# Norm products, token-major transposes and softmax transposes written one projection later, and pinned in their place, in a two-layer hybrid backbone

## The chip, the cores and the metric

The kernel runs on one core of one Trainium2 chip. The metric is the device time of one execution in microseconds (us).

## What is computed

A stream of 512 latent tokens and 256 context tokens, 1024 channels wide, goes through two layers. In each, a modulated RMSNorm is followed by one wide input projection that feeds three mixers side by side, and by a squared-ReLU MLP. All values are float32; the large products are made as three products of rounded and remainder parts.

```
h    = rmsnorm(x) * (1 + sc) + sh
na_* , dn_*, z, fn_u, gate = split(h @ w_in)
o_na = softmax(q k_window^T + bias | q k_ctx^T) v        # 8 heads of 64, 8x16 window and all context
q,k  = rope(l2norm(silu(conv5(dn_q,k)))), v = silu(conv5(dn_v))
o_dn = headnorm(delta_rule_fwd + delta_rule_bwd) * silu(z)   # 4 heads of 128
o_fn = real(fft2(fn_u))
x    = x + gt1 * (sum_i sigmoid(gate_i) * (o_i @ w_i)) @ w_out
x    = x + gt2 * relu(norm(x) @ w1)^2 @ w2
```

The first layer computes latents and context (an "all" projection is 512 + 256 columns); in the second, queries, z and gates are needed for the latents alone.

## The kernel before

Weights come in blocks of 128 output channels. `wload` (L224) loads two halves of 256 KB on SyncE's queue, rounds them on ScalarE (`whi`, L232) and makes the remainder on GpSimd or VectorE (`wlo`, L235). `proj` (L239) runs 24 matmuls over the latents and 24 over the context (L244). `inproj` (L378) does one block of the input projection in one go; its two results take both buffers of PSUM tag `pl`.

Each layer has three parts: a Fourier part (head 0 of the delta rule runs beside it), the mixing part, and the rest (branch projections, output projection, MLP). The mixing part is four Python generators that `by_clock` (L329) interleaves while the program is written out: each `yield` tells how many units of a planned clock the step takes, and the stream with the earliest due time writes its next step.

- `stream_in`: the remaining projections, 40 per layer. A projection yields `IN_T`, 12 units in the first layer and 7 in the second. It picks attention inputs first, then delta heads (when the head two before is over), then z; a gate projection is put in at a fixed ratio.
- `stream_na`: attention, four blocks of two heads; `na_in` of the next block starts when the block before is done. `na_pair` (L786) is one tile of 128 queries: scores (yield 1), softmax (yield 3), transposes of the probabilities on TensorE (L814, yield 2), product with v (L820, yield 2). A block is six pairs in the first layer, four in the second.
- `stream_prep`: for one head after the other, the triangular inverses (`dn_prep`): products of k and q (L553, L555), 31 substitution steps on VectorE (L580, L582), two round trips through DRAM, four rounds of small matmuls, and the copy that ends it (L642). A head begins when its `qT` is written.
- `stream_dn`: the scan of each head (`dn_step`), then its output (`dn_out`, L725).

`dn_in` (L511) prepares one head: project k, convolution and SiLU (`conv_silu`, L455: evacuation L460, five VectorE steps, a sigmoid, the product L470), L2 norm and rotation (`l2_rope`, L473: square L476, product with ones on TensorE L481, four DMAs that swap rows, a product on GpSimd L493, the sum L495); then k's token-major transposes (`tok_major`, L504), project v, convolution; v's transposes, project q, convolution, L2 norm. The convolution's padded input `cin`, its result `y`, the square `r_l2` and a gate's `gl` all take buffers of SBUF tag `cy`, of which the mixing part has three (`mix_a`, L954).

The writing order is a priority, not the final order. When the program is built, a scheduler fills each engine's queue: of what it estimates to be ready, the earliest written goes first; `PRI` moves the delta scan 200 places forward in the first layer. On the chip each queue runs in the order so fixed, and an instruction waits at its head until its inputs are there. So a matmul that was put too early holds everything behind it on TensorE.

Of the kernel before, what the change touches and what calls it, by code (L numbers as in the profile page):

```python
# [17 lines left out]
P = 128  # L18
D = 1024
KD = 8  # L20
TL = 512
TC = 256
TT = TL + TC
# [9 lines left out]


IN_T, LAT_STEP, HEAD, PRI, GR, G0 = (12, 7), (2, 3), (5, 0), (200, 0), (0.5, 0.3), (0, 1)

ADA_G, ADA_BR, ADA_WO, ADA_M = 0.5, 0.3, 1.5, 0.95

# [4 lines left out]
V_N1, V_N2, V_BADA, V_CONV, V_DNN, V_LEN = 0, 8, 16, 64, 124, 125  # L43
# [3 lines left out]
def kernel(ctx: ExitStack, tc: tile.TileContext, A: dict, out: bass.AP):  # L47
# [316 lines left out]
    def layer(l):  # L364
# [13 lines left out]
        def inproj(t, sg):  # L378
# [13 lines left out]
                proj(pc, w, KD, hh, hl, sg[1:], TL, k0)  # L392
            return pl, pc

        def evac(dst, ps):
            act.copy(dst[:, 0:TL], ps[0])  # L396
            if ps[1] is not None:
                act.copy(dst[:, TL:TT], ps[1][:, 0:TC])
# [74 lines left out]
        def l2_rope(y, w, scale, name, par):  # L473
            n = 770 if w > TL else 512
            r = U("r_l2", tag="cy", w=774)
            act.activation(out=r[:, :n], in_=y[:, :n], func=AF.Square)  # L476
            for s0, s1, o0 in ((0, TL, 0), (TL, TT, 514)):
                if s0 < w:
                    o1 = o0 + s1 - s0
                    ps = ps_aux("ps_l2")  # L480
                    pe.matmul(ps[:, 0:s1 - s0], lhsT=ones, rhs=r[:, o0:o1], start=True, stop=True)  # L481
                    act.activation(out=r[:, o0:o1], in_=ps[:, 0:s1 - s0], func=AF.Ln, bias=EPS)
                    act.activation(out=r[:, o0:o1], in_=r[:, o0:o1], func=AF.Exp, scale=-0.5)
            o = U(name, tag=name + par)
# [12 lines left out]

        def tok_major(src, offs, name, tag):

            o = U(name, tag=tag).rearrange("p (j e) -> p j e", e=P)  # L500
            for j0, j1 in ((0, 4), (4, 6)):
                ps = ps_aux("ps_tm")
                for j in range(j0, j1):
                    pe.transpose(ps[:, (j - j0) * P:(j - j0 + 1) * P], src[:, offs[j]:offs[j] + P], ident)  # L504
                act.copy(o[:, j0:j1], ps[:, 0:(j1 - j0) * P].rearrange("p (j e) -> p j e", e=P))
            return o

# [1 line left out]
        OFFY = [j * P for j in range(4)] + [514, 642]  # L509

        def dn_in(h, st):  # L511
            y = conv_silu(inproj(T_DNK + h, ALL), V_CONV + 5 * (4 + h), TT)
            st["kT"] = l2_rope(y, TT, 1.0, "kT", str(h % 2))
            yield IN_T[l]
            st["ktok"] = tok_major(st["kT"], OFF, "ktok", f"ktok{h % 2}")
            y = conv_silu(inproj(T_DNV + h, ALL), V_CONV + 5 * (8 + h), TT)
            yield IN_T[l]
            st["vtok"] = tok_major(y, OFFY, "vtok", f"vtok{h % 2}")
            y = conv_silu(inproj(T_DNQ + h, segs), V_CONV + 5 * h, W)
            st["qT"] = l2_rope(y, W, float(P) ** -0.5, "qT", str(h % 2))  # L520
            yield IN_T[l]

        def dn_prep(h, st):
            kT, qT = st["kT"], st["qT"]
# [172 lines left out]
                else:  # L697
                    dve.tensor_tensor(O, O, ps[:, 0:P], op=ALU.add)

        def dn_z(h):  # L700
            ps = inproj(T_Z + h, segs)
            zz = U("zz", tag="zz")
            sg = tp.tile([P, TT], F32, tag="t3", name="sgz")
            evac(zz, ps)
            sigmoid_into(sg[:, :W], zz[:, :W])
            dve.tensor_tensor(zz[:, :W], sg[:, :W], zz[:, :W], op=ALU.mult)
            return zz

        def dn_out(h, st):
            O, zz = st["O"], st["zz"]  # L710
# [20 lines left out]

        def pre_gates():
            for k in range(NPRE):
                ps = inproj(T_GATE + k, segs)
                sg = tp.tile([P, TT], F32, tag="t3", name="sgp")
                gl = U("gl", tag="cy", w=774)
                evac(gl, ps)
                sigmoid_into(sg[:, :W], gl[:, :W])
                sp.dma_start(out=gpre[k, :, :W], in_=sg[:, :W])
                yield IN_T[l]  # L740


        ona = drp.tile([4, P, TT], F32, tag="ona", bufs=1, name="ona")
# [1 line left out]
        def na_in(c, st):  # L745

            halves = (slice(0, 64), slice(64, P))
            ps = inproj(T_NAK + c, ALL)
            raw = tp.tile([P, TT], F32, tag="t3", name="kraw")
            act.copy(raw[:, 0:TL].rearrange("p (t r c) -> p t r c", t=4, c=16),  # L750
                     ps[0].rearrange("p (r t c) -> p t r c", r=8, c=16))
# [2 lines left out]
            for t, r, r2 in zip(ks, halves, halves[::-1]):  # L754
                act.copy(t[r], raw[r])
                dve.tensor_tensor(t[r2], raw[r], t[r].bitcast(F32), op=ALU.subtract)
            yield IN_T[l]
            ps = inproj(T_NAV + c, ALL)
# [5 lines left out]
            yield IN_T[l]  # L764
            ps = inproj(T_NAQ + c, segs)
# [18 lines left out]
            yield IN_T[l]  # L784

        def na_pair(scores, n_loc, biases, vts, dst, view):  # L786

# [4 lines left out]
            for ps, bias in zip(pss, biases):  # L792
# [15 lines left out]
                dve.reciprocal(s4[:, 5:6], s4[:, 3:4])  # L808
                dve.tensor_scalar(Pm[:, :nk], Pm[:, :nk], s4[:, 5:6], None, op0=ALU.mult)
                Ps.append(Pm)  # L810
            yield 3
            for ps, Pm in zip(pss, Ps):
                for i in range(nk // P):
                    pe.transpose(ps[:, i * P:(i + 1) * P], Pm[:, i * P:(i + 1) * P], ident)  # L814
                act.copy(Pm[:, :nk], ps[:, :nk])
            yield 2
            for i, v in enumerate(vts):
                for hh, Pt in enumerate(Ps):
                    f = slice(64 * hh, 64 * hh + 64)
                    pe.matmul(pss[0][f, 0:P], lhsT=v[:, f], rhs=Pt[:, i * P:(i + 1) * P], start=(i == 0),  # L820
                              stop=(i == nk // P - 1), tile_position=(0, 64 * hh))
            act.copy(dst, view(pss[0][:, 0:P]))
            yield 2

# [126 lines left out]
                    yield 2  # L951


        mix_a = scope("mixa", **{f"{n}{i}": 1 for n in ("kT", "qT", "ktok", "vtok") for i in range(2)}, O=1, zz=1, cy=3)  # L954
        mix_a.__enter__()

        sts = [{} for _ in range(NDH)]
# [31 lines left out]
        def stream_in():  # L989
            dn, na, zq, gs = list(range(1, NDH)), list(range(NDH)), list(range(1, NDH)), pre_gates()  # L990
            n = ng = 0
            run = None
            while dn or na or zq or run or ng < NPRE:
                if ng < min(NPRE, GR[l] * n + G0[l]):
                    ng += 1
                    yield next(gs)
                    continue
                if run is None:
                    heads = sum("over" in st for st in sts)
                    todo = {"d": dn and heads > dn[0] - 2, "z": zq and "out" in sts[zq[0] - 1],  # L1000
                            "n": na and (na[0] == 0 or "done" in nas[na[0] - 1])}
                    for t in "ndz":
                        if todo[t]:
                            break
                    else:
                        if not (dn or na or zq):
                            ng += 1
                            yield next(gs)
                        else:
                            yield 2  # L1010
                        continue
                    if t == "d":
                        h = dn.pop(0)
                        run = dn_in(h, sts[h])
                    elif t == "n":
                        h = na.pop(0)
                        run = na_in(h, nas[h])
                    else:
                        h = zq.pop(0)
                        sts[h]["zz"] = dn_z(h)  # L1020
                        n += 1
                        yield IN_T[l]
                        continue
                try:
                    yield next(run)
                    n += 1
                except StopIteration:
# [5 lines left out]
        layer.psf = None  # L1033
        with scope("fn", ue=8, uz=4, fa=24, dftc=1):
            cur["dve_lo"] = 2
            gates()
            fg, dg = fourier(), dn_in(0, sts[0])
            for g in (dg, fg, dg, fg, dg, fg, fg):
                next(g)
            for _ in fg:  # L1040
                pass
            sts[0]["zz"] = dn_z(0)
# [310 lines left out]
```

## Time and profile before

| | |
|---|---|
| median of 3 runs | 2690.07 us (2690.01 to 2692.57) |
| profiled execution, own time | 2695.4 us |
| its span, first to last instruction | 2693.6 us |
| mean granted TensorE clock | 0.967 |

Busy time of an engine is the union of its instructions; a row of waits names the instruction at the head of the queue, who released it, the total in us, how often, and the longest. "Granted clock" is the share of TensorE's full 2.4 GHz; 0.5 is 1.2 GHz. The mixing part of the first layer lies at about 150 to 754 us, that of the second at 1652 to 2164 us, with the Fourier parts just before them.

### The profile page before, as it was taken

How to read it: one execution, taken by the hardware profiler on the slowest of the kernel's cores; microseconds unless marked ns; L12 is line 12 of the kernel's file. 1: busy time of each engine (PE TensorE's matmuls, PEld its weight loads, DVE VectorE, ACT ScalarE, POOL GpSimd, SP SyncE). 2: the span in 40 equal slices, each digit the busy share in tenths (PEclk: the TensorE clock that was granted, in tenths of full speed). 3: DMA queues.
4: the chain of work that ended last, by engine and by line, in shares of the span. 5: the costliest groups of instructions: out<-in, count | busy, mean ns of one | idle time of the engine just before them, and what ended most of it. 6: DMA issues, size and time to landing. Idle time of an engine off the chain costs nothing. (4 is left out here: it accounts for less than half of the span.)

```text
span 2693.6 us, 39422 instructions
## 1 busy us (share of the span) xinstructions
PE 2490.9 (92%) x14608; PEld 2049.6 (76%) x14608; DVE 1599.0 (59%) x3207; ACT 1185.0 (44%) x2453; POOL 649.8 (24%) x536
## 2 busy tenths in 40 slices
PE   6988989899998989999999989888989999999998
PEld 3876867677886868888888867666767777788886
DVE  5647686758479999532323365768778457433334
ACT  4546556555653224121212255455555663423333
POOL 3221212231121113111111133222233232222222
PEclk8998999999998999999999999998989999999999
DMA  6222222222166665522222213222232346233332
GB/s 219 73 82 66 67 70 67 74 76 64 67 200 211 223 197 187 180 63 63 63 64 65 88 59 99 70 79 65 70 87 65 99 122 200 78 95 98 94 95 89
DMA packets 186249, 275.68 MB, mean 102 GB/s; under 512 B 57364, under 2 KB 77592, under 8 KB 185928
## 3 DMA queue, kind: packets, MB, share of 16 engines
q1 hardware_dynamic: 186056, 273.16, 33.3%
q8 instruction: 115, 1.88, 0.3%
q14 instruction: 78, 0.64, 0.1%
HBM read 242.86 MB, written 26.03 MB: 100 GB/s over the span
## 5 line engine op out<-in xcount | busy, mean ns | idle before, releaser
L235 POOL TENSOR_TENSOR wlo<-wr,whi 128x512 fp32r<-128x512 f32 x352 | 499.3, 1420 | 1683.5 <-ACT whi L232 1589.9
L232 ACT CAST whi<-wr 128x512 fp32r<-128x512 f32 x544 | 334.9, 619 | 723.7 <-PE ps_m L244 470.5
L244 PE MATMUL ps_in<-hh,whi 128*128 128x512 f32 x960 | 380.5, 407 | 13.8 <-ACT kraw L750 7.3
L244 PE MATMUL ps_in<-hh,wlo 128*128 128x512 f32 x960 | 377.4, 404 | 5.3 <-DVE wlo L235 3.4
L244 PE MATMUL ps_in<-hl,whi 128*128 128x512 f32 x960 | 378.0, 404 | 0.0
L244 PE MATMUL ps_m<-ml,whi 128*128 128x512 f32 (+1 forms) x768 | 233.8, 358 | 4.4 <-POOL ml L312 3.9
L244 PE MATMUL ps_m<-mh,whi 128*128 128x512 f32 (+1 forms) x768 | 232.7, 358 | 4.4 <-ACT mh L308 4.4
L244 PE MATMUL ps_m<-ah,whi 128*128 128x512 f32 (+1 forms) x776 | 233.7, 354 | 3.2 <-ACT ah L251 3.2
L235 DVE TENSOR_TENSOR wlo<-wr,whi 128x512 fp32r<-128x512 f32 x192 | 133.6, 696 | 172.3 <-ACT whi L232 170.9
L244 PE MATMUL ps_m<-ah,wlo 128*128 128x512 f32 (+1 forms) x776 | 234.9, 356 | 0.0
L244 PE MATMUL ps_m<-al,whi 128*128 128x512 f32 (+1 forms) x776 | 233.9, 355 | 0.6 <-DVE al L252 0.6
L244 PE MATMUL ps_m<-mh,wlo 128*128 128x512 f32 (+1 forms) x768 | 232.8, 356 | 0.0
L244 PEld LDWEIGHTS ps_in<-hh,whi 128*128 128x128 f32 x960 | 182.5, 194 | 46.9 <-ACT kraw L750 7.6
L244 PEld LDWEIGHTS ps_in<-hh,wlo 128*128 128x128 f32 x960 | 180.9, 193 | 40.1 <-DVE wlo L235 4.4
L244 PEld LDWEIGHTS ps_in<-hl,whi 128*128 128x128 f32 x960 | 181.7, 194 | 30.9 <-issue 2.1
L1187 DVE SCALAR_TENSOR_TENSOR x<-ps_m,mod,x 128x512 f32<-128x512 f32 (+1 forms) x97 | 60.8, 654 | 229.6 <-PE ps_m L244 229.6
L173 DVE SCALAR_TENSOR_TENSOR jada<-wada,csb 128x1024 f32<-128x1024 f32 x128 | 174.6, 1364 | 13.3 <-DMA wada<-in_wat_dram 11.9
L244 PE MATMUL ps_inc<-hh,whi 128*128 128x256 f32 x512 | 150.5, 294 | 0.3 <-ACT gl L396 0.3
L244 PEld LDWEIGHTS ps_m<-ml,whi 128*128 128x128 f32 x768 | 127.8, 190 | 29.6 <-POOL ml L312 6.9
L244 PEld LDWEIGHTS ps_m<-mh,whi 128*128 128x128 f32 x768 | 128.0, 190 | 28.2 <-ACT mh L308 6.5
L244 PE MATMUL ps_inc<-hh,wlo 128*128 128x256 f32 x512 | 148.8, 291 | 0.0
L244 PE MATMUL ps_inc<-hl,whi 128*128 128x256 f32 x512 | 148.7, 290 | 0.0
(339 smaller groups left out, 5032.9 us busy)
## 6 DMA issues: line engine op xcount, KB each, us to landing
wr<-in_w_dram SPq DMA_DIRECT2D x256, 256.0 KB
wr<-in_wi_dram SPq DMA_DIRECT2D x224, 256.0 KB
wada<-in_wat_dram SPq DMA_DIRECT2D x80, 512.0 KB
wr<-in_wb_dram SPq DMA_DIRECT2D x48, 256.0 KB
wada<-in_wa_dram SPq DMA_DIRECT2D x32, 256.0 KB
wr<-in_wo_dram SPq DMA_DIRECT2D x32, 256.0 KB
gpre<-sgp SPq DMA_DIRECT2D x16, 384.0 KB
sgg<-gpre SPq DMA_DIRECT2D x16, 384.0 KB
```

The costliest lines, as they stand in the source:

```text
L173: dve.scalar_tensor_tensor(junk, in0=w, scalar=1.0, in1=cur["csb"][:, v * D:v * D + D], op0=ALU.mult, op1=ALU.mult, accum_out=MOD[l][:, 4 ...
L232: act.copy(hi, raw)
L235: eng.tensor_tensor(lo, raw, hi.bitcast(F32), op=ALU.subtract)
L244: pe.matmul(ps[:, s0 - off:s1 - off], lhsT=a, rhs=b[k][:, s0:s1], start=(k == 0 and i == 0), stop=(k == kn - 1 and i == 2))
L1187: dve.scalar_tensor_tensor(x2[k][:, s0:s1], in0=ps[:, s0:s1], scalar=mod(l, 5, k, v), in1=x2[k][:, s0:s1], op0=ALU.mult, op1=ALU.add)
```

## The change

- `inproj_g` replaces `inproj` inside the mixing part: a projection is written in two pieces (latents, half of the contraction each) and, where there is context, a third piece; after each but the last a tuple yields the piece's share of `IN_T`, so the whole takes the same planned time.
- `dn_in` writes k's L2 norm after v's projection, k's and v's token-major transposes after q's projection, and q's L2 norm after whichever projection follows (`tails` and `flush` in `stream_in`). In the Fourier part (`cur["whole"]`) the same order holds with projections whole.
- `na_pair` yields 6 instead of 3 ahead of the transposes and 3 instead of 2 after them.
- The first norm product, the first transpose of each group and the first product with v are pinned (`keep_in_program_order`): an edge of issue order, not a wait, that keeps the instruction behind the TensorE instruction written just before it.
- Tag `cy` of the mixing part has five buffers instead of three. z becomes a generator like the others.

```diff
+NA_T = (6, 3)
+        def inproj_g(t, sg):
+            if cur["whole"]:
+                return inproj(t, sg)
+            w = wload(A["wi"][l, t])
+            pl, pc = ps_aux("ps_in", "pl"), None
+            proj(pl, w, KD, hh, hl, LAT, 0, 0, KD // 2)
+            yield (in_t(sg),)
+            proj(pl, w, KD, hh, hl, LAT, 0, KD // 2)
+            if len(sg) == 2:
+                yield (in_t(sg),)
+                pc = ps_aux("ps_inc", "pl")
+                proj(pc, w, KD, hh, hl, sg[1:], TL)
+            return pl, pc
+        def in_t(sg):
+            return IN_T[l] / (1 if cur["whole"] else 1 + len(sg))
...
-                    pe.matmul(ps[:, 0:s1 - s0], lhsT=ones, rhs=r[:, o0:o1], start=True, stop=True)
+                    t = pe.matmul(ps[:, 0:s1 - s0], lhsT=ones, rhs=r[:, o0:o1], start=True, stop=True)
+                    if s0 == 0:
+                        tc.keep_in_program_order(t)
...
         def dn_in(h, st):
-            y = conv_silu(inproj(T_DNK + h, ALL), V_CONV + 5 * (4 + h), TT)
+            y = conv_silu((yield from inproj_g(T_DNK + h, ALL)), V_CONV + 5 * (4 + h), TT)
+            yield in_t(ALL)
+            ps = yield from inproj_g(T_DNV + h, ALL)
             st["kT"] = l2_rope(y, TT, 1.0, "kT", str(h % 2))
-            yield IN_T[l]
+            y = conv_silu(ps, V_CONV + 5 * (8 + h), TT)
+            yield in_t(ALL)
+            ps = yield from inproj_g(T_DNQ + h, segs)
             st["ktok"] = tok_major(st["kT"], OFF, "ktok", f"ktok{h % 2}")
-            y = conv_silu(inproj(T_DNV + h, ALL), V_CONV + 5 * (8 + h), TT)
-            yield IN_T[l]
             st["vtok"] = tok_major(y, OFFY, "vtok", f"vtok{h % 2}")
-            y = conv_silu(inproj(T_DNQ + h, segs), V_CONV + 5 * h, W)
+            y = conv_silu(ps, V_CONV + 5 * h, W)
+            yield in_t(segs)
             st["qT"] = l2_rope(y, W, float(P) ** -0.5, "qT", str(h % 2))
-            yield IN_T[l]
...
-            yield 3
+            yield NA_T[0]
             for ps, Pm in zip(pss, Ps):
                 for i in range(nk // P):
-                    pe.transpose(ps[:, i * P:(i + 1) * P], Pm[:, i * P:(i + 1) * P], ident)
+                    t = pe.transpose(ps[:, i * P:(i + 1) * P], Pm[:, i * P:(i + 1) * P], ident)
+                    if i == 0:
+                        tc.keep_in_program_order(t)
                 act.copy(Pm[:, :nk], ps[:, :nk])
-            yield 2
+            yield NA_T[1]
...
-        mix_a = scope("mixa", **{f"{n}{i}": 1 for n in ("kT", "qT", "ktok", "vtok") for i in range(2)}, O=1, zz=1, cy=3)
+        mix_a = scope("mixa", **{f"{n}{i}": 1 for n in ("kT", "qT", "ktok", "vtok") for i in range(2)}, O=1, zz=1, cy=5)
...
+                x = yield from piece(run)
+                if x is None:
+                    run = None
+                    continue
+                n += 1
+                yield x
+                flush()
+                if t == "d" and "ktok" in sts[h]:
+                    tails.append(run)
+                    run = None
+            flush()
```

## Rows read from the trace of the kernel before

**Rows 1.** The page, busy us of each engine, share of the span, instructions.

```profile
PE 2490.9 (92%) x14608; PEld 2049.6 (76%) x14608; DVE 1599.0 (59%) x3207; ACT 1185.0 (44%) x2453; POOL 649.8 (24%) x536
```

**Rows 2.** Stretches: length, busy PE, PEld, DVE, ACT, POOL, granted clock, DMA share, GB/s.

```profile
150.00:754.00 604.00, 551.19 (x3899) 456.62 (x3898) 408.76 (x1054) 339.13 (x783) 143.90 (x125) 0.96 0.25 72
1600.00:1652.00 52.00, 47.58 (x248) 39.21 (x247) 29.75 (x46) 28.23 (x64) 14.11 (x18) 0.97 0.33 87
1652.00:2164.00 512.00, 452.38 (x3045) 356.37 (x3045) 359.89 (x944) 289.95 (x681) 149.19 (x125) 0.94 0.28 78
```

**Rows 3.** TensorE's waits, whole span: who waited for whom, total, times, longest.

```profile
PE ps_s L814 <- DVE Pm L809: 30.4, 23, 6.9
...
PE ps_l L481 <- ACT r_l L476: 13.0, 9, 3.5
PE ps_tm L504 <- DVE kT L495: 10.0, 6, 3.0
```

**Rows 4.** TensorE's waits in the first layer's mixing part (150 to 754 us).

```profile
PE ps_s L814 <- DVE Pm L809: 12.2, 12, 3.6
PE ps_l L481 <- ACT r_l L476: 8.7, 4, 3.5
```

**Rows 5.** TensorE's waits in the second layer's mixing part (1652 to 2164 us).

```profile
PE ps_s L814 <- DVE Pm L809: 18.1, 11, 6.9
PE ps_tm L504 <- DVE kT L495: 5.8, 3, 2.6
```

**Rows 6.** Timeline around the longest wait: start, us, engine, line [idle before, releaser].

```profile
1823.56 0.59 ACT L460 COPY cin<-ps_in 128x512 f32<-128x512 f32 x1 [0.20 <-PE ps_in L244]
...
1844.58 0.28 PE L244 MATMUL ps_inc<-hh,wlo 128*128 128x256 f32 x1
...
1849.98 0.94 DVE L470 TENSOR_TENSOR cy<-cy,cin 128x770 f32<-128x770 f32 x1
...
1850.96 0.84 ACT L476 ACTIVATE r_l<-cy 128x770 f32<-128x770 f32 x1 [1.28 <-DVE cy L470]
1850.98 0.17 POOL L459 MEMSET cin<- 128x2 f32 x3 [4.19 <-DVE cy L470]
...
1851.71 0.57 ACT L460 COPY cin<-ps_in 128x512 f32<-128x512 f32 x1
1851.76 0.45 PE L814 MATMUL ps_s<-ident,Pm 128*128 128x128 f32 x1 [6.90 <-DVE Pm L809]
```

**Rows 7.** GpSimd's waits, whole span: the convolution's border fill.

```profile
POOL cin L459 <- DVE cy L470: 62.7, 8, 22.4
```

**Rows 8.** Chain of waits, cut to one undisturbed latent projection: start, us, count.

```profile
2186.55 5.44 PE ps_in L244 x24
```

**Rows 9.** Attention results leaving PSUM: one block, second layer, first and last pair.

```profile
1711.08 0.27 ACT L822 COPY o_na<-ps_s 128x128 f32<-128x128 f32 x1 [1.32 <-PE ps_s L820]
...
1759.71 0.27 ACT L822 COPY o_na<-ps_s 128x128 f32<-128x128 f32 x1
```

**Rows 10.** A stretch around one wait of 3.5 us, columns as in Rows 2.

```profile
236.00:248.00 12.00, 8.49 (x36) 5.23 (x36) 6.24 (x19) 8.00 (x19) 1.73 (x4) 0.72 0.20 47
```

**Rows 11.** A stretch with transposes alone counted: length, busy PE, PEld, granted clock, DMA.

```profile
1874.00:1880.00 6.00, 2.18 (x14) 1.70 (x14) 1.00 0.37 85
```

**Rows 12.** VectorE's timeline, second layer: heads' qT (L495), end of inverses (L642), output (L725).

```profile
1899.72 0.68 DVE L495 TENSOR_TENSOR qT<-kn,rot 128x512 f32<-128x512 f32 x1
1900.33 0.55 DVE L642 COPY L<-N 128x768 f32<-128x768 f32 x1
...
2035.01 1.65 DVE L495 TENSOR_TENSOR qT<-kn,rot 128x512 f32<-128x512 f32 x1
...
2161.49 0.75 DVE L725 SCALAR_TENSOR_TENSOR o_dn<-ps_ot,vecs,zz 128x512 f32<-128x512 f32 x1 [1.21 <-PE ps_ot L724]
```

**Rows 13.** End of the first layer's mixing part: last attention result, last gate.

```profile
688.22 0.28 ACT L822 COPY o_na<-ps_sc 128x128 f32<-128x128 f32 x1
...
752.37 0.96 DVE L127 SCALAR_TENSOR_TENSOR sgp<-gl,sgp 128x768 f32<-128x768 f32 x1 [6.93 <-ACT sgp L126]
```

More of the change, by code (lines that the diff above doesn't have):

```diff
@@ L503, in tok_major @@
                 for j in range(j0, j1):
-                    pe.transpose(ps[:, (j - j0) * P:(j - j0 + 1) * P], src[:, offs[j]:offs[j] + P], ident)
+                    t = pe.transpose(ps[:, (j - j0) * P:(j - j0 + 1) * P], src[:, offs[j]:offs[j] + P], ident)
+                    if j == 0:
+                        tc.keep_in_program_order(t)
                 act.copy(o[:, j0:j1], ps[:, 0:(j1 - j0) * P].rearrange("p (j e) -> p j e", e=P))
@@ L698, in dn_step, with dn_z @@
                     dve.tensor_tensor(O, O, ps[:, 0:P], op=ALU.add)
-        def dn_z(h):
-            ps = inproj(T_Z + h, segs)
+        def dn_z(h, st):
+            ps = yield from inproj_g(T_Z + h, segs)
             zz = U("zz", tag="zz")
@@ L706, in dn_z @@
             dve.tensor_tensor(zz[:, :W], sg[:, :W], zz[:, :W], op=ALU.mult)
-            return zz
+            st["zz"] = zz
+            yield in_t(segs)
         def dn_out(h, st):
@@ L733, in pre_gates @@
             for k in range(NPRE):
-                ps = inproj(T_GATE + k, segs)
+                ps = yield from inproj_g(T_GATE + k, segs)
                 sg = tp.tile([P, TT], F32, tag="t3", name="sgp")
@@ L739, in pre_gates @@
                 sp.dma_start(out=gpre[k, :, :W], in_=sg[:, :W])
-                yield IN_T[l]
+                yield in_t(segs)
         ona = drp.tile([4, P, TT], F32, tag="ona", bufs=1, name="ona")
@@ L747, in na_in @@
             halves = (slice(0, 64), slice(64, P))
-            ps = inproj(T_NAK + c, ALL)
+            ps = yield from inproj_g(T_NAK + c, ALL)
             raw = tp.tile([P, TT], F32, tag="t3", name="kraw")
@@ L756, in na_in @@
                 dve.tensor_tensor(t[r2], raw[r], t[r].bitcast(F32), op=ALU.subtract)
-            yield IN_T[l]
-            ps = inproj(T_NAV + c, ALL)
+            yield in_t(ALL)
+            ps = yield from inproj_g(T_NAV + c, ALL)
             vN = tp.tile([P, TT], F32, tag="t3", name="vN")
@@ L763, in na_in @@
             vt = tok_major(vN, OFF, "naV", tag="n")
-            yield IN_T[l]
-            ps = inproj(T_NAQ + c, segs)
+            yield in_t(ALL)
+            ps = yield from inproj_g(T_NAQ + c, segs)
             raw = tp.tile([P, TT], F32, tag="t3", name="qraw")
@@ L783, in na_in @@
             st.update(ks=ks, vt=vt, qd=qd, ql=ql)
-            yield IN_T[l]
+            yield in_t(segs)
         def na_pair(scores, n_loc, biases, vts, dst, view):
@@ L810, in na_pair @@
                 Ps.append(Pm)
[L811 removed]
+            yield NA_T[0]
             for ps, Pm in zip(pss, Ps):
                 for i in range(nk // P):
[L814 removed]
+                    t = pe.transpose(ps[:, i * P:(i + 1) * P], Pm[:, i * P:(i + 1) * P], ident)
+                    if i == 0:
+                        tc.keep_in_program_order(t)
                 act.copy(Pm[:, :nk], ps[:, :nk])
[L816 removed]
+            yield NA_T[1]
             for i, v in enumerate(vts):
@@ L819, in na_pair @@
                     f = slice(64 * hh, 64 * hh + 64)
-                    pe.matmul(pss[0][f, 0:P], lhsT=v[:, f], rhs=Pt[:, i * P:(i + 1) * P], start=(i == 0),
-                              stop=(i == nk // P - 1), tile_position=(0, 64 * hh))
+                    t = pe.matmul(pss[0][f, 0:P], lhsT=v[:, f], rhs=Pt[:, i * P:(i + 1) * P], start=(i == 0),
+                                  stop=(i == nk // P - 1), tile_position=(0, 64 * hh))
+                    if i == hh == 0:
+                        tc.keep_in_program_order(t)
             act.copy(dst, view(pss[0][:, 0:P]))
@@ L992, in stream_in, with flush, piece @@
             run = None
+            tails = []
+            def flush():
+                while tails:
+                    next(tails.pop(), None)
+            def piece(g):
+                while True:
+                    x = next(g, None)
+                    if not isinstance(x, tuple):
+                        return x
+                    yield x[0]
             while dn or na or zq or run or ng < NPRE:
@@ L995, in stream_in @@
                     ng += 1
-                    yield next(gs)
+                    yield (yield from piece(gs))
+                    flush()
                     continue
@@ L1005, in stream_in @@
                     else:
+                        flush()
                         if not (dn or na or zq):
                             ng += 1
-                            yield next(gs)
+                            yield (yield from piece(gs))
                         else:
@@ L1019, in stream_in @@
                         h = zq.pop(0)
[L1020 to L1027, printed above, removed]
-                    run = None
+                        run = dn_z(h, sts[h])
+                x = yield from piece(run)
+                if x is None:
+                    run = None
+                    continue
+                n += 1
+                yield x
+                flush()
+                if t == "d" and "ktok" in sts[h]:
+                    tails.append(run)
+                    run = None
+            flush()
         psf = layer.psf or psum("psf", pl=2, pa=2, fb=4)
@@ L1035, in layer @@
             cur["dve_lo"] = 2
+            cur["whole"] = True
             gates()
@@ L1039, in layer @@
                 next(g)
+            next(dg, None)
             for _ in fg:
                 pass
-            sts[0]["zz"] = dn_z(0)
+            next(dn_z(0, sts[0]))
+            cur["whole"] = False
         psf.__exit__(None, None, None)
```

## The prediction, made before the changed kernel was built

> **What bounds the kernel now.** I read the shares of busy time first. TensorE is busy for 92% of the span [rows 1], so the whole is near TensorE's own work, and only idle time and slow clock can be won back. Next the stretches, to see where these lie: the first layer's mixing part has 604.0 - 551.2 = 52.8 us without a matmul, the second's 512.0 - 452.4 = 59.6 us [rows 2]. Both run below the full clock: 0.96 and 0.94, so (1 - 0.96) x 604 = 24 us and (1 - 0.94) x 512 = 31 us of clock are not granted. VectorE is busy for 68% and 70% there; it is no bound on the average, but it is full for microseconds at a time. The change touches the mixing parts and the Fourier parts ahead of them, nothing else.
>
> Then TensorE's waits, by line. Three of the longest belong to lines that the change moves: softmax transposes on the normalised probabilities, 30.4 us in 23 waits; norm products on their squares, 13.0 us in 9; k's transposes on the rotated k, 10.0 us in 6 [rows 3]. Together 53.4 us, 2.0% of the span. By part, the transposes wait 12.2 us in the first and 18.1 us in the second layer, the norm products mostly in the first, k's transposes mostly in the second [rows 4, 5].
>
> The timeline shows what such a wait is made of [rows 6]. TensorE ends v's projection at 1844.9 and stands until 1851.76 at a transpose whose probabilities are late. It could have taken another projection, but had no room for it: the result of the last one is evacuated only at 1851.71. That copy waits for a padded buffer, whose border GpSimd fills at 1850.98, and GpSimd had waited 4.19 us for the product that ends k's convolution (L470). With `cin`, `y` and a square or a gate alive, the three `cy` buffers are all taken. GpSimd stands in this place for 62.7 us, eight times [rows 7]. So two causes meet: an instruction put too early, and PSUM held back by the third buffer.
>
> **The change, part by part.** The sum is made against the profiled execution's 2695.4 us.
>
> *Softmax transposes.* They are written 6 instead of 3 planned units after the softmax and can't float ahead. A unit is worth 604/480 = 1.26 us in the first and 512/284 = 1.80 us in the second layer (the stream of projections is written out in 480 and 284 units). So 3.8 and 5.4 us of other work come in between, against a mean wait of 30.4/23 = 1.3 us and a longest of 6.9. Nearly all is covered while projections are at hand; with five buffers they are more often. I take three quarters: -23 us, between 0 and -30.
>
> *Norm products.* The position gains little: from the evacuation to the square takes 27.4 us here (1823.56 to 1850.96, [rows 6]), and one projection, 5.44 us over the latents [rows 8], was written in between in effect already. What gains is the two more buffers, by which the next evacuation and so the next projection go ahead. -9 us, between 0 and -13.
>
> *k's transposes.* They now have v's and q's projections between them and the end of k's convolution, with the four row-swapping DMAs, the GpSimd product and the sum under it. The longest wait, 3.0 us, is less than one latent projection. -8 us, between 0 and -10.
>
> *Clock.* Around a wait of 3.5 us the granted clock was 0.72 over 12 us, and TensorE was busy in 8.5 us of them [rows 10]: 0.28 x 8.5 = 2.4 us lost beside the wait itself. Waits on the three lines are the largest ones in most of the slow stretches, but not in all. Five such losses out of the 24 + 31 us: -12 us, between 0 and -29.
>
> *What rides along.* The split in pieces adds no matmul and no load: the weight loads, two of 256 KB a projection, are issued at the first piece. SyncE's queue meets the k rotation's four DMAs later, behind v's and q's weights; k isn't needed until the inverses start, so that costs nothing while q comes later still. GpSimd's queue loses the border fills' waits, behind which weight remainders queued; I leave that at nothing, since the projections [rows 8] run without a gap when weights are ahead. On ScalarE the evacuation of v now stands behind k's norm in writing order; its wait is the buffer's, which is gone. New edges of order are no waits, but a pinned instruction that is late holds all matmuls behind it, as before.
>
> *q's norm.* It is written behind one more projection. In the second layer the inverses wait for q: head 2's `qT` at 1899.72, where the inverses before end at 1900.33, and head 3's at 2035.01; the end of head 3's inverses, its scan and its output at 2161.49 close the part [rows 12]. So what delays q there delays the end. One latent projection is 5.44 us, for two heads 10.9 us at most; the convolution ahead of the norm takes longer than that, so most is hidden: +3 us, between -5 (q's projection itself comes earlier) and +11.
>
> *A longer attention stream.* A pair takes 12 planned units instead of 8. Taking the stream with the earliest due time through all yields, attention ends at 524 instead of 410 units in the first layer, where the projections end at 502 instead of 480; in the second at 304 instead of 240, and the scan's last step moves from 274 to 314. In the first layer attention ended at 688.2 and the last gate at 752.4 [rows 13]; that slack of 64 us is used up and some 22 units follow with no projection under them. +8 us, between 0 and 22 x 1.26 = 28. In the second layer the planned delay doesn't turn into time one for one: a pair takes (1759.7 - 1711.1)/3 = 16.2 us on the chip [rows 9], or 9 units, not 8, with waits in it, and idle places of the plan are filled with later projections. Eight pairs lie ahead of head 3's projections; I take under a microsecond each: +6 us, between 0 and (314 - 274) x 1.80 = 72.
>
> The sum: -23 - 9 - 8 - 12 + 3 + 8 + 6 = -35 us. 2695.4 - 35 = 2660.4 us for a profiled execution. The median of the runs lay 5.3 us below the profiled one; the same distance gives **2655 us**.
>
> **The rivals.**
>
> *Attention becomes the bound (slower).* Place: second layer, from the start of a block of attention to the next head's projections, which the plan puts behind it. For: head 3's inverses start at 220 planned units instead of 180, and q was just in time or late before [rows 12]. Against: a pair took 9 units of time before [rows 9]; the plan only comes nearer to the chip. Price: if the 40 units cost 60 of their 72 us, the sum becomes -35 - 6 + 60 = +19: about 2710 us. It decides from about 41 us on, some 5 us for each of the eight pairs.
>
> *The waits move on (no difference).* The probabilities, squares and rotated k come from VectorE and ScalarE at the same time as before; TensorE then stands before products with v, `dn_prep`'s first products or an evacuation. For: VectorE's 70% in the second layer [rows 2], and the wait there ends with VectorE. Against: L470's wait on buffers [rows 7] is removed and not moved. The waits give back as much as the stream costs: about 2688 us.
>
> *Transposes slow the clock wherever they stand.* In the trace, six microseconds in which 14 transposes take 2.18 us have the full clock [rows 11]. The clock term then doesn't come: 2655 + 12 = 2667 us.
> The Trainium skill, "TensorE: Matmul & The Clock Gate", Part 4 (PE-mode transpose), says that the full clock doesn't engage for transposes, as they don't count as a busy array. By that rule this rival holds; the trace disagrees where transposes stand among projections.
>
> *All of it comes back.* Waits 53 us and clock 29 us gone, with nothing added: about 2608 us.
>
> **How the numbers follow.** Forecast, between 2625 and 2680: 0.54. Clock stays down, 2667: 0.10. All comes back: 0.05. No difference: 0.11. Attention as the bound: 0.20. A change of 0.2%, 5.4 us, is about what a measurement of this kernel can tell from none. So faster 0.54 + 0.10 + 0.05 = 0.69, same 0.11, slower 0.20. The range runs from 2615, which leaves out most of the best case, to 2708, which leaves out over half of the worst.
>
> **What would show it.** Right: the waits on L809, L476 and L495 in [rows 3] fall to about 13 us together; GpSimd's on L470 [rows 7] to near nothing; mixing parts of about 580 and 500 us at clocks of 0.98 and 0.96. q's step is right if head 3's `qT` comes no later after 1652 than now. Attention as the bound would show as pairs over 20 us and a late third or fourth `qT`; a tail in the first layer as an attention result behind the last gate. Wrong altogether if the norm products wait as long with five buffers, since I put their cause there, or if lines that I left out (L553 to L562, L830, L831) take over the waits.

## The result

| | before | after |
|---|---|---|
| median | 2690.04 us (4 runs) | 2760.24 us (4 runs; 2752.46 to 2765.57) |
| ratio, with its 95% interval | | 1.0262 (1.0232 to 1.0292) |
| span of the profiled execution | 2693.6 us | 2750.6 us |
| mean granted TensorE clock | 0.967 | 0.955 |

The change makes the kernel 2.6% slower. The forecast was 2655 us, between 2615 and 2708; the time lies above the range.

Lines have moved: softmax transposes are now L843 (before: L814), the product with v L851 (L820), the normalised probabilities L837 (L809), the norm product L501 (L481), k's transposes L526 (L504), the copy that ends the inverses L669 (L642).

The first row of the page of the changed kernel, against [rows 1]:

```profile
PE 2497.6 (91%) x14608; PEld 2068.6 (75%) x14608; DVE 1633.8 (59%) x3207; ACT 1183.9 (43%) x2453; POOL 638.5 (23%) x536
```

The same instructions. The profiled executions are 57.0 us apart, the medians 70: in the profile TensorE's busy time grew by 6.7 us and its idle time by 50.3, from 202.7 to 253.0. TensorE's waits in the changed kernel, whole span, against [rows 3]:

```profile
PE ps_kk L580 <- DVE PT L589: 23.7, 6, 10.6
PE ps_r L628 <- DMA Tst<-wd: 21.1, 5, 12.9
...
PE ps_s L863 <- DVE qd L808: 17.5, 10, 3.8
PE ps_s L843 <- DVE Pm L837: 12.8, 11, 2.2
...
PE ps_l L501 <- ACT r_l L496: 9.2, 3, 5.8
...
PE ps_tm L526 <- DVE kT L517: 7.3, 3, 4.4
```

The three waits that the change was argued from fell from 53.4 to 29.3 us. Two new ones of 44.8 us stand above them: the inverses' second product (L580), and the first matmul behind the substitution (L628), which waits for a DMA; before they were 1.9 us and nothing. But 29.3 + 44.8 is only 21 us more than 53.4, and TensorE is idle for 50.3 us more. The rest is spread over waits on lines that the change doesn't move: attention's scores on their query (L863), say, 17.5 us in place of 3.7. Such a list names the instruction at the head of the queue; it doesn't say why that one stands there and not another. Stretches of the changed kernel (length, busy PE, PEld, DVE, ACT, POOL, clock, DMA share, GB/s), against [rows 2]:

```profile
150.00:754.00 604.00, 519.01 (x3622) 432.38 (x3621) 407.04 (x997) 312.84 (x721) 138.01 (x121) 0.92 0.23 65
...
450.00:550.00 100.00, 70.95 (x516) 59.65 (x514) 72.41 (x159) 50.12 (x100) 24.00 (x22) 0.79 0.25 70
```

and the second of these in the kernel before:

```profile
450.00:550.00 100.00, 90.40 (x673) 74.31 (x673) 74.54 (x204) 49.71 (x113) 19.44 (x20) 0.97 0.26 71
```

In these 100 us TensorE is busy 19.5 us less, and at a clock of 0.79 it loses, by my estimate, another 0.21 x 71 = 15 us (before 0.03 x 90 = 3). That is some 31 us in one stretch, most of what the first layer loses. The timeline says why. Attention results, the last gate of the first layer, and the second layer's last head output in the changed kernel, against [rows 12, 13]:

```profile
421.36 0.27 ACT L855 COPY o_na<-ps_s 128x128 f32<-128x128 f32 x1
...
528.62 0.27 ACT L855 COPY o_na<-ps_s 128x128 f32<-128x128 f32 x1 [0.28 <-PE ps_s L851]
...
787.49 0.96 DVE L129 SCALAR_TENSOR_TENSOR sgp<-gl,sgp 128x768 f32<-128x768 f32 x1 [0.18 <-ACT sgp L128]
...
795.00 0.27 ACT L855 COPY o_na<-ps_sc 128x128 f32<-128x128 f32 x1 [1.20 <-PE ps_sc L851]
...
2217.61 0.75 DVE L753 SCALAR_TENSOR_TENSOR o_dn<-ps_ot,vecs,zz 128x512 f32<-128x512 f32 x1 [1.21 <-PE ps_ot L752]
```

The first pair of a block leaves at 421.36, the second at 528.62, 107 us later; in the kernel before, these two left 10 us apart. The last gate comes 35 us later than before, the last attention result, before 64 us ahead of it, now 7.5 us behind it; the second layer's end is 56 us late. So 35 to 43 us are lost in the first layer's mixing part and 13 to 21 behind it.

What the second pair waited for, on ScalarE and TensorE in the changed kernel:

```profile
461.37 1.21 ACT L846 COPY Pm<-ps_s 128x512 f32<-128x512 f32 x2
...
520.40 0.31 PE L628 MATMUL ps_r<-Tst,N 32*32 32x32 f32 x2 [12.86 <-DMA Tst<-wd]
522.61 1.49 PE L628 MATMUL ps_r<-Tst,N 32*32 32x32 f32 x46 [1.89 <-DMA Tst<-wd]
...
526.57 1.98 PE L851 MATMUL ps_s<-Pm,naV 128*64 128x128 f32 x16
```

The pair's transposed probabilities have left PSUM at 462.6. The pinned product with v (L851) runs 64 us later, right behind the inverses' small products (L628, and L638 and L642 that follow it), of which the first waits for the substitution's result. TensorE had little else in its queue at the end of this time: the projections alone, busy PE and PEld, in the changed kernel:

```profile
500.00:565.00 65.00, 7.55 (x45) 6.56 (x43) 0.63 0.20 55
```

These are 7.55 us of projections in 65 us, where the kernel before has 34.16. By the program, the next block's attention inputs are written when the block before is done; that this is why they are missing here isn't shown by a run of its own. A pinned softmax transpose shows the same; VectorE and TensorE:

```profile
211.16 0.47 DVE L837 TENSOR_SCALAR Pm<-Pm,s 128x512 f32<-128x512 f32 x1
...
257.42 0.79 PE L699 MATMUL ps_ch<-vtok,L 128*128 128x128 f32 x2 [3.45 <-DVE L L669]
...
260.57 0.63 PE L721 MATMUL ps_ch<-Uc,PT 128*128 128x128 f32 x2
260.99 1.06 PE L843 MATMUL ps_s<-ident,Pm 128*128 128x128 f32 x4
```

The probabilities are ready at 211.6; their transposes run 49.4 us later, right behind a product of the scan (L721), which had to wait for the inverses' last copy (L669). In between TensorE ran projections in the main, so no wait names the transposes. I measured this as lateness: over the 80 groups of transposes, the time from the end of L837 to the first transpose. It sums to 39.4 us before, with no group over 8 us, and to 421.6 us after, with 12 groups (six pairs) over 8 us. The first transposes of these pairs stand right behind the scan's L721 (three) or L703 (two), or the inverses' L580 (one). The products with v are late in the same way: from the end of a pair's last copy (L846) to its first product it is 1.0 us in sum before and 128.6 after, with three pairs over 8 us.

So the theory: a pin ties an instruction to the TensorE instruction *written* just before it. The planned clock mixes four streams, so that is often a matmul of the scan or the inverses, which runs long after its place in the writing. Rivals: the longer units alone (the prediction's own rival), and that an edge of order costs wherever it is tied.

### The profile page after: what moved, and what is told of

The parts are those of the page before. It is cut to its first block, busy times and chain, and to the rows that moved or that the text cites. A ratio compares the mean times of both kernels' runs of the same rounds, so it can differ in the third digit from the quotient of the medians.

```text
span 2750.6 us, 39430 instructions
## 1 busy us (share of the span) xinstructions
PE 2497.6 (91%) x14608; PEld 2068.6 (75%) x14608; DVE 1633.8 (59%) x3207; ACT 1183.9 (43%) x2453; POOL 638.5 (23%) x536
## 5 line engine op out<-in xcount | busy, mean ns | idle before, releaser
L237 POOL TENSOR_TENSOR wlo<-wr,whi 128x512 fp32r<-128x512 f32 x352 | 488.6, 1390 | 1720.6 <-ACT whi L234 1606.0
L246 PEld LDWEIGHTS ps_m<-ah,whi 128*128 128x128 f32 x776 | 128.5, 189 | 27.2 <-ACT ah L253 4.5
```

Of the source, the lines that this page charges most:

```text
L237: eng.tensor_tensor(lo, raw, hi.bitcast(F32), op=ALU.subtract)
L246: pe.matmul(ps[:, s0 - off:s1 - off], lhsT=a, rhs=b[k][:, s0:s1], start=(k == 0 and i == 0), stop=(k == kn - 1 and i == 2))
```

## The experiments

All ratios are to the kernel before, run on the same chip, with a 95% interval. A run's waits and lateness come from its one profiled execution.

**No pins.** The changed kernel without its four edges.

```diff
-tc.keep_in_program_order(t)
+pass
```

> The changed kernel without its pins: order of writing, pieces, planned units and five buffers stay. Pins theory (a pinned transpose or product with v stands behind whatever TensorE instruction was written before it, often a matmul of the scan or the inverses that is late): the softmax transposes, which came up to 49 us after their probabilities, come within 8 us, and most of the 70 us goes: 2670 to 2705 us. Longer-stream theory (12 planned units a pair instead of 8 make attention the end): it stays above 2735 us and the last attention result stays some 100 us later than before in the first layer. Pieces theory (the split makes TensorE stand 10.6 us at the second round of head 0's products, in both layers): that wait stays and some 20 us of the loss with it.

Measured: 2695.72 us, ratio 1.0045 (1.0023 to 1.0067). Lateness falls to 46.4 us, no group over 8 us. Of the 2.6%, 1.0262 - 1.0045 = 2.2% are the pins'. The stretch of 100 us from above, and two waits:

```profile
450.00:550.00 100.00, 93.89 (x719) 76.20 (x718) 78.06 (x203) 66.71 (x158) 34.23 (x24) 1.00 0.31 84
```

```profile
PE ps_kk L580 <- DVE PT L589: 24.9, 6, 11.5
PE ps_s L843 <- DVE Pm L837: 16.9, 18, 2.0
```

The hole is gone: 44.63 us of projections run between 500 and 565, and the second pair of that block leaves 44.5 us behind the first. But the kernel isn't faster than before, and the wait at L580 is there without pins.

**The pins tied elsewhere.** The same four edges, but to the last matmul of the projection written last.

```diff
-tc.keep_in_program_order(t)
+pin_proj(t)      # an edge of order, no wait, to cur["mm"], which proj() sets
```

> The changed kernel with the pins tied to the projection matmul written last, and not to TensorE's instruction written last. The position behind the projection pieces is kept; the tie to scan and inverses is gone. Pins theory: as without pins, 2655 to 2700 us, and if holding the place is worth what was meant by it, some 10 us faster than without pins. Longer-stream theory: above 2735 us, since the planned units are the same.

Measured: 2698.64 us, 1.0037 (1.0020 to 1.0055), lateness 60.6 us, one group over 8 us (11.0, behind a projection). As many edges on the same instructions cost nothing that can be measured when their other end is a projection. The 10 us that holding the place might have won didn't come. This decides between the theory and the rival of the edge itself.

**Which pins.** First the changed kernel with attention's two pins taken away; then the kernel before with these two pins alone.

```diff
 # after:
-                        tc.keep_in_program_order(t)      # transposes; the same for the product with v
+                        pass
 # before:
+                    if i == 0:
+                        tc.keep_in_program_order(t)      # transposes; the same for the product with v
```

> Only attention's two pins are taken out; norm products and token-major transposes stay pinned. If it is attention's pins: within 15 us of the kernel without any pin. If the norm products' and k's transposes' pins harm as much (they too stand behind late scan steps): above 2720 us.

> The kernel before with attention's two pins and nothing else. Pins theory: softmax transposes come tens of us after their probabilities, right behind scan matmuls; ratio 1.01 to 1.03. If the pins only harm along with the longer planned units or the pieces: under 1.005.

Measured: 2715.25 us, 1.0095 (1.0069 to 1.0121), and 2744.01 us, 1.0220 (1.0193 to 1.0247). Attention's pins cost 1.0262 - 1.0095 = 1.7% in the changed kernel and 2.2% by themselves; those on norms and token-major transposes 1.0095 - 1.0045 = 0.5%. The first run lies between what I expected: 19.5 us above the kernel without pins, not 15, and under 2720. How much of attention's price is the transposes' and how much the products' no run separates. With the pins alone lateness is 394.5 us (the products with v: 93.4); its longest, on VectorE and TensorE:

```profile
355.37 0.49 DVE L809 TENSOR_SCALAR Pm<-Pm,s 128x512 f32<-128x512 f32 x1
...
412.00 0.19 PE L611 MATMUL ps_w<-N,R 32*32 32x32 f32 x1
412.01 0.19 PE L615 MATMUL ps_w<-R,N 32*32 32x32 f32 x1
412.13 1.09 PE L814 MATMUL ps_s<-ident,Pm 128*128 128x128 f32 x8
```

The 56.3 us end with the last of the inverses' small products (L615), and three of the five late pairs stand behind that line, where I had expected the scan's matmuls; one stands behind the scan (L676), one behind a norm product (L481). Here a part of the loss does show as waits, but on other lines:

```profile
PE ps_l L481 <- ACT r_l L476: 52.6, 11, 12.5
...
PE ps_r L601 <- DMA Tst<-wd: 18.6, 2, 16.9
```

Before these were 13.0 us and nothing. The instruction that is late isn't the one that the list names.

**Longer units.** The kernel before with 6 and 3 planned units in `na_pair`; the changed kernel without pins and with 3 and 2; the changed kernel without pins and with whole projections (units of 6 and 3).

```diff
 # before:
-            yield 3
+            yield 6
-            yield 2
+            yield 3
 # after, no pins:
-NA_T = (6, 3)
+NA_T = (3, 2)
 # after, no pins, another kernel:
-            cur["whole"] = False
+            cur["whole"] = True
```

> The kernel before with 6 and 3 planned units for 3 and 2, and nothing else. Longer-stream theory, my second rival: slower, ratio 1.005 to 1.02, with a late third and fourth qT in the second layer. Forecast's reading: fewer waits on the probabilities (30.4 us before) and no loss, ratio 0.99 to 1.0.

> The changed kernel without pins and with the old planned units 3 and 2; pieces stay. Units theory: attention in the first layer no longer ends behind the last gate (762 us beside 752 without pins), ratio under 1.001. Pieces theory: the 25 us of waits at ps_kk stay, and the ratio stays between 1.002 and 1.006.

> The changed kernel without pins and with every projection written in one go; order of dn_in, planned units 6 and 3, five buffers stay. Without pins 0.45% of the loss was left. Pieces theory: with pieces, TensorE stands 10.6 us at head 0's second k product (ps_kk behind PT) at the start of both mixing parts; written whole, those waits (25 us in all) fall under 5 us and 10 to 20 us come back: a ratio of 0.997 to 1.001 to the kernel before. Units theory (what is left comes from the longer planned attention): the waits may go, the ratio stays at 1.003 or more.

Measured: 1.0115 (1.0088 to 1.0142); 0.9991 (0.9974 to 1.0007); 1.0099 (1.0070 to 1.0127). Longer units cost 1.15% alone and 1.0045 - 0.9991 = 0.54% beside the pieces. Where, in the kernel before with longer units alone, against [rows 13]:

```profile
775.27 0.96 DVE L127 SCALAR_TENSOR_TENSOR sgp<-gl,sgp 128x768 f32<-128x768 f32 x1 [0.18 <-ACT sgp L126]
...
783.28 0.27 ACT L822 COPY o_na<-ps_sc 128x128 f32<-128x128 f32 x1 [1.21 <-PE ps_sc L820]
```

Attention ends behind the last gate. The third and fourth qT of the second layer are late as expected (by 21.9 and 14.7 us), but its first was late by 30.5 us already: what is lost is lost in the first layer. The run with the old units has the time of the kernel before: order, pieces and buffers together give nothing that can be measured. Whole projections cost another half per cent beside the longer units (1.0099 against 1.0045), though they have no long wait at L580 (4.3 us). So that wait isn't what is lost beside the longer units; why pieces help there and not beside the old units no run shows.

**Buffers, order, pieces.** The kernel before with five `cy` buffers; the changed kernel without pins, with the old units, and every projection whole, so that only order and buffers are left.

```diff
 # before:
-O=1, zz=1, cy=3)
+O=1, zz=1, cy=5)
 # after, no pins, NA_T = (3, 2):
-            cur["whole"] = False
+            cur["whole"] = True
```

> The kernel before with five cy buffers and nothing else. The prediction put the norm products' waits (13.0 us) and GpSimd's 62.7 us behind L470 on the third buffer. If that is right: the norm products wait under 5 us, GpSimd's wait goes, and 10 to 25 us are won, 2665 to 2680 us. If VectorE's own work sets these times: 2685 to 2695 us with the waits moved elsewhere.

> The kernel with the change, without pins, with the old units of attention (3 and 2), and every projection whole: what is left of the change is the later place of norms and token-major transposes in the writing order, and five buffers. Theory: the new place alone takes the waits of the norm products and of k's transposes from 23 us to under 12, but does nothing for the softmax transposes, whose wait stays above 20 us; ratio 0.995 to 1.000, and what the kernel with pieces adds to that (0.999 with the wait at the inverses) is about nothing. Rival, that the pieces are what gains: the norm products still wait 10 us and more, and the ratio is 1.002 to 1.006, since whole projections cost half a per cent beside the longer units too.

Measured: 2681.52 us, 0.9982 (0.9965 to 0.9999), and 2682.33 us, 0.9990 (0.9974 to 1.0007). With five buffers alone GpSimd and TensorE wait for

```profile
POOL cin L459 <- DVE cy L470: 5.7, 2, 4.5
```

```profile
PE ps_l L481 <- ACT r_l L476: 12.6, 8, 3.5
```

against 62.7 us in [rows 7] and 13.0 us in [rows 3]: the border fill no longer waits, and the norm products wait as long as ever. The buffers weren't their cause, and 0.2% is won, 5 us, not 10 to 25. Nor is it the order alone; TensorE's waits with order and buffers:

```profile
PE ps_s L843 <- DVE Pm L837: 19.4, 22, 2.3
...
PE ps_l L501 <- ACT r_l L496: 16.3, 7, 5.6
...
PE ps_tm L526 <- DVE kT L517: 6.2, 4, 2.6
```

My expectation of under 12 us for the last two fails with 22.5; the time came as I expected it. Written one projection later, the norm product waits as long; with pieces it waits 8.0 us. Why the pieces shorten it I didn't settle.

**What the pieces cost.** In the run without pins and with old units the wait at L580 is 21.6 us, two times, once at the start of each mixing part. VectorE and TensorE at the first:

```profile
150.50 0.60 DVE L564 TENSOR_SCALAR Dl<-Df,g_gc 128x128 f32<-128x128 f32 x2 [9.92 <-DMA Df<-gdr]
```

```profile
154.12 0.28 PE L246 MATMUL ps_inc<-hh,wlo 128*128 128x256 f32 x1
164.91 0.80 PE L580 MATMUL ps_kk<-kT 128*128 128x128 f32 x2 [10.50 <-DVE PT L589]
```

VectorE gets the decay rows from DRAM only at 150.5, and 14 us pass until it has read the first product. The second product needs that one's PSUM buffer, and with pieces it comes to the head of the queue at 154.4: TensorE stands for 10.5 us in the middle of a projection. Cure: the first two projections of a part whole.

```diff
+                cur["whole"] = n < 2
                 x = yield from piece(run)
```

> The kernel with the change, without pins, with the old units of attention (3 and 2), and the first two projections of each mixing part written whole; the later ones stay in pieces. Theory: TensorE's new wait of some 11 us at the second product of the inverses, at the start of both mixing parts (21.6 us in two), is made by the pieces, which let that product come to the head of the queue before the decay rows have landed from DRAM; with a whole projection ahead of it the wait falls under 6 us for both parts, the other waits stay (softmax transposes 15 to 20 us), and the time falls by 12 to 22 us to a ratio of 0.990 to 0.995. Rival: the wait is not made by the pieces but by the product of the earlier order, or TensorE only stands elsewhere in its place: the ratio stays at 0.997 to 1.001.

Measured: 2677.71 us, 0.9971 (0.9958 to 0.9984). TensorE's second product, and two waits:

```profile
161.98 0.52 PE L580 MATMUL ps_kk<-kT 128*128 128x128 f32 x2 [0.31 <-DVE PT L589]
```

```profile
PE ps_s L843 <- DVE Pm L837: 25.0, 19, 6.7
...
PE ps_l L501 <- ACT r_l L496: 5.7, 3, 3.5
```

The second product comes to the head at 161.7, 7 us later. Its wait is gone (L580 in all: 3.9 us), and the kernel is 0.3% faster than the kernel before. But against 0.9991 with all in pieces the gain is 0.2%, which the two intervals don't tell from none, of the 0.5 to 0.8 that I expected: this is the rival's end of the range. TensorE does stand elsewhere for a good part of it. The transposes wait 25.0 us in place of 16.7, and the projection behind the first product waits for a PSUM buffer that ScalarE reads (8.2 us on this line in place of 1.5):

```profile
158.31 0.80 PE L246 MATMUL ps_in<-hh,whi 128*128 128x512 f32 x1 [5.53 <-ACT kraw L778]
```

**Later transposes without the harm.** Two versions of this kernel: with the transposes tied to the last projection matmul, and with 4 units ahead of them.

```diff
 # one:
-                        pass
+                        pin_proj(t)      # edge to cur["mm"], as above, transposes only
 # other:
-NA_T = (3, 2)
+NA_T = (4, 2)
```

> The kernel with the change, with the old units of attention, the first two projections of a mixing part whole and only one pin left: the first transpose of each group of probabilities is tied to the last matmul of the projection written last, not to the instruction written just before it. Theory: a projection runs nearly in the order in which it is written, so that this tie costs nothing and takes a part of the 25.0 us for which the transposes wait for their probabilities without it: wait 12 to 20 us, no group more than 8 us behind its probabilities, ratio 0.992 to 0.998 to the kernel before. Rival, that an edge of order costs by itself wherever it is tied: groups over 8 us late come back and the ratio is 1.005 and more.

> The kernel with the change, without pins, the first two projections of a mixing part whole, and 4 instead of 3 planned units ahead of the softmax transposes (2 behind them, as before the change). Theory: what longer units cost is paid where attention ends behind the last projections of the first layer, at 6 units; at 4 it still ends before the last gate (about 715 against 750 us), so that only the gain is left: the wait for probabilities falls from 25.0 to 12 to 20 us, ratio 0.993 to 0.998. Rival, that every added unit costs in the second layer by later heads: ratio 0.999 to 1.003, with head 3's q later than 2010 us.

Measured: 2676.86 us, 0.9966 (0.9954 to 0.9979), and 2674.72 us, 0.9958 (0.9944 to 0.9972). The tie brings the wait for probabilities to 17.2 us and the time to no visible change; lateness is 39.3 us, none over 8: again an edge costs nothing by itself. With 4 units the wait for the probabilities, the last attention result and the last gate of the first layer, and the stretches of [rows 2] read

```profile
PE ps_s L843 <- DVE Pm L837: 18.0, 21, 2.1
```

```profile
695.75 0.27 ACT L855 COPY o_na<-ps_sc 128x128 f32<-128x128 f32 x1 [0.44 <-PE ps_sc L851]
...
752.12 0.96 DVE L129 SCALAR_TENSOR_TENSOR sgp<-gl,sgp 128x768 f32<-128x768 f32 x1 [6.93 <-ACT sgp L128]
```

```profile
150.00:754.00 604.00, 550.15 (x3893) 453.95 (x3892) 404.47 (x1054) 339.45 (x783) 141.58 (x125) 0.96 0.25 71
1652.00:2164.00 512.00, 455.94 (x3123) 364.97 (x3122) 370.81 (x951) 298.52 (x703) 159.07 (x131) 0.96 0.29 82
```

Attention ends 56 us ahead of the last gate, and head 3's `qT` comes at 2002.3, so the rival of later heads doesn't hold. This is the lowest ratio: 0.4%, 11 us, below the kernel before and 3.0% below the changed one. The intervals of the last three versions overlap, so which of them is best isn't shown. Its second layer has 3.6 us more TensorE work done by 2164 than [rows 2], at a clock of 0.96 instead of 0.94.

## Why the prediction was wrong

The ladder, each rung adding to the one above it:

| kernel | ratio | step |
|---|---|---|
| order and five buffers | 0.9990 | -0.1% |
| + pieces | 0.9991 | 0.0 |
| + units of 6 and 3 | 1.0045 | +0.54% |
| + pins on norms and token-major transposes | 1.0095 | +0.50% |
| + pins on attention (the change) | 1.0262 | +1.67% |

The steps depend on the order of the rungs: longer units cost 1.15% alone, attention's pins 2.2% alone, and pieces give back half a per cent beside the longer units and nothing beside the old ones.

- *The step that failed is one sentence of what rides along:* "New edges of order are no waits, but a pinned instruction that is late holds all matmuls behind it, as before." It asks what stands behind the pinned instruction, not what it is tied to, and so the edges stand in the sum at nothing. The edge holds the pinned one behind a predecessor that may be late itself. Its price is 0.50 + 1.67 = 2.17%, 58 of the 70 us by which the kernel is slower. That the scan and the inverses are streams of their own, written in between by the planned clock, was known ahead; I didn't ask which of them a pin would be tied to.
  The Trainium skill, "PSUM — Partial Sum Buffer", section "Engine vs sequencer instructions", says that matmuls start and complete in program order. The row at 520.40 agrees: in the 12.86 us ahead of it TensorE stood for one matmul, and the product with v, whose probabilities had been there since 462.6, didn't pass it.
- *Softmax transposes, -23:* the wait on their probabilities did fall, 30.4 to 12.8 us, and to 18.0 us with 4 units. The later place isn't the whole cause of it: with the old units and no pins the wait was 16.7 to 25.0 us too, with longer units alone 20.7. And the wait says nothing of the time, since pinned transposes are late without a wait of their own.
- *Norm products, -9:* the wait fell to 9.2 us, but the cause given, the third buffer, is wrong: five buffers leave it at 12.6, which the prediction itself had named as the sign. [Rows 6] showed two waits that end together, and I took the one for the cause of the other.
- *k's transposes, -8:* 10.0 to 7.3 us. The size was off.
- *Clock, -12:* it went the other way, 0.92 and 0.93 in the two parts. Without pins it is 0.97 and 0.92: in the first layer it went down where the pins made holes; in the second it hardly moved with them (0.94 before), and what holds it down there stays open. With 4 units it is 0.96 and 0.96.
- *Pieces at no cost:* right for the time beside the old units (0.9990 without, 0.9991 with), wrong for the reason. The wait at L580 (L553 before) was 1.9 us and is 23.7 us, and other waits became shorter. The prediction counted the matmuls and loads of a split projection, not what may now slip in between its pieces.
- *Attention stream, +14:* sound in place. The first layer's tail came as described, and 0.54% is 14.5 us beside the pieces; alone it was 31 us, above the forecast's value and inside its ends.
- *q's norm, +3:* its price isn't told apart by a run. Its sign holds: with order and buffers head 3's `qT` comes at 2003.9, before at 2035.0.
- *Rivals.* "Attention becomes the bound" had the sign, and pairs of the second layer do take longer (27 us in its first block, against 16.2 in [rows 9]), but most of the loss lies in the first layer, and the longer units are its lesser cause; alone they lengthen the first layer and not the second. "Transposes slow the clock" isn't what happened: without pins the 100 us stretch from 450 has the full clock, and in the slowest part of the hole, 530 to 565 us, transposes and the like (matmuls with the identity) are 5.84 of TensorE's 24.06 busy us. "All comes back" assumed that 53 us of wait are 53 us of time. In the kernel with the first projections whole the three waits are 25.0 + 5.7 + 4.7 = 35.4 us, 18 us less, and the time is 8 us less.

The chances gave "slower" 0.20, all on one mechanism. The pins had no rival of their own; a sentence on what each is tied to would have been one.

## What to carry to other kernels

Before an edge of order is added, ask what its other end is: tied to the last instruction *written*, in a program that mixes several streams, it inherits that stream's lateness. The list of waits then names other lines or none; what shows it is the gap between an input that is ready and the instruction that uses it. Tied to the projections, the same edges cost nothing here. And when a long block is split, look at what can slip in between its parts.

## What the runs showed of the hardware

Between 530 and 565 us of the changed kernel, attention's matmuls and the inverses' small ones ran and no projection (columns as in Rows 2):

```profile
530.00:565.00 35.00, 24.06 (x129) 17.10 (x129) 17.82 (x62) 17.99 (x58) 5.39 (x3) 0.57 0.05 15
```

The granted clock was 0.57, close to the lower of its two levels, though TensorE was busy for 24.06 of the 35 us. Without pins, with projections ahead of it and in it, this stretch had 1.00. Before, I had counted the clock as a loss around single waits of a few microseconds; in this hole in the supply of projections it was low for tens.
